# Reordering the last pair of a matmul kernel: one third product and the direct columns moved ahead, final block added and stored in two halves

## The chip, the cores and the metric

The kernel runs on one core of one Trainium2 chip. The metric is the device time of one execution in microseconds. Beside it stands the span of a profiled execution, which is some 1.8 us shorter (363.13 against 361.35 us for the profiled run of before). The profiled run can lie above the median of the timed ones, as here (363.13 against 362.59 us).

## The reference

```python
def setup_inputs():
    batch, seq, hidden = 16, 512, 768
    return {
        "x": np.random.randn(batch, seq, hidden).astype(np.float32),
        "w_qkv": np.random.randn(hidden, 3 * hidden).astype(np.float32),
    }

def reference(x, w_qkv):
    qkv = np.matmul(x, w_qkv)
    hidden = x.shape[-1]
    q, k, v = qkv[..., :hidden], qkv[..., hidden:2*hidden], qkv[..., 2*hidden:]
    return np.stack([q, k, v], axis=0).astype(np.float32)
```

That is 8192 rows of x by 768, times a 768 x 2304 matrix. The output, 75.5 MB, is split into three.

## The kernel before

The rows are worked in 32 pairs of 128-row tiles. Of the 2304 columns, 2048 are done in two "quads" (a and b) of 2 x 512 columns. A quad is a block product with seven products in place of eight; product n is `do(u, n)`. The other 256 columns, the "direct" ones, are plain products (`rem`). Within a quad, products 1, 6, 7 and 4 accumulate one after another in the same PSUM bank `u.x` (PSUM is the memory that the products are written to), and ScalarE reads that bank between them; 5 and 3 share `u.y`; VectorE adds.

```python
    def do(u, n):
        ...
        elif n == 7:
            product(u, 7, u.x, False)
            nc.scalar.activation(c22, u.x[:], ident)
            nc.vector.tensor_tensor(c22, c22, u.y[:], op=add)
        elif n == 4:
            product(u, 4, u.x, False)
            nc.scalar.activation(c21, u.x[:], ident)
        elif n == 3:
            product(u, 3, u.y, False)
            nc.vector.tensor_tensor(c12, c12, u.y[:], op=add)
```

The last pair has a function of its own, which stores each block as soon as it is done. A block is 128 x 512 values, 256 KB. `store_cols` makes two stores of 128 KB of it where it crosses from one output tensor to the next.

```python
        def rem_stored(r):
            ps = bank()
            rem_row(p, r, ps[:, :REM])
            o = or_pool.tile([P, 2, REM], fp32, name="orem")
            nc.scalar.activation(o[:, 0, :], ps[:, :REM], ident)
            row = (2 * p + r) * P
            nc.scalar.dma_start(out_flat[1, row:row + P, ...], o[:, 0, :])   # cut

        do(a, 1); do(b, 1); do(a, 2); do(a, 6); do(b, 2); do(b, 6)   # lines joined
        for u in (a, b):
            store_cols(u, 0, 0, CB, nc.sync)
        for u in (a, b):
            do(u, 5)
            do(u, 7)
            store_cols(u, 1, CB, 2 * CB, nc.sync)
        do(a, 4)
        store_cols(a, 1, 0, CB, nc.scalar)
        rem_stored(0)
        do(b, 4)
        store_cols(b, 1, 0, CB, nc.scalar)
        for u in (a, b):
            do(u, 3)
            store_cols(u, 0, CB, 2 * CB, nc.sync)
        rem_stored(1)
```

Of the kernel before, what the change touches and what calls it, by code (L numbers as in the profile page):

```python
# [10 lines left out]
def kernel(  # L11
# [20 lines left out]
    nc = tc.nc  # L32
# [10 lines left out]
    CB = 512  # L43
# [7 lines left out]
    add = mybir.AluOpType.add  # L51
# [149 lines left out]
    def product(u, n, ps, start):  # L201
        t1, t2, t3, t4 = ts[u.q]
        if n <= 2:
            h = (n - 1) * KH
            lhs = [xb[u.p][:, h + j, :P] for j in range(KH)]
            rhs = [b1[u.q][:, h + j, :] for j in range(KH)]
        else:
            k, t = {3: (4, b22[u.q][:]), 4: (0, t4), 5: (1, t1), 6: (2, t2), 7: (3, t3)}[n]
            lhs = [sr[u.p][:, k, j, :] for j in range(KH)]
            rhs = [t[:, j, :] for j in range(KH)]  # L210
        for j in range(KH):
            nc.tensor.matmul(  # L212
                ps[:], lhs[j], rhs[j],
                start=(start and j == 0), stop=(j == KH - 1), skip_group_check=True,
            )

    def bank():
        return ps_pool.tile([P, CB], fp32, name="ps")

    def do(u, n):  # L220
        c11, c12 = u.o[:, 0, :CB], u.o[:, 0, CB:]
        c21, c22 = u.o[:, 1, :CB], u.o[:, 1, CB:]
        if n == 1:
            u.x = bank()
            product(u, 1, u.x, True)
            nc.scalar.activation(c11, u.x[:], ident)  # L226
        elif n == 2:
            u.z = bank()
            product(u, 2, u.z, True)
            nc.vector.tensor_tensor(c11, c11, u.z[:], op=add)  # L230
        elif n == 6:
            product(u, 6, u.x, False)
            nc.scalar.activation(c12, u.x[:], ident)  # L233
        elif n == 5:
            u.y = bank()
            product(u, 5, u.y, True)
# [10 lines that stand above are left out]
# [13 lines left out]
    def rem_row(p, r, ps):  # L260
        for j in range(KT):
            nc.tensor.matmul(  # L262
                ps, xb[p][:, j, r * P:(r + 1) * P], w_rem[j // KH][:, j % KH, :],
                start=(j == 0), stop=(j == KT - 1), skip_group_check=True,
            )
# [30 lines left out]
    def store_cols(u, r, lo, hi, eng):  # L296

        c = Q_OFF[u.q] + lo
        end = Q_OFF[u.q] + hi
        while c < end:  # L300
            n = min(end, (c // H + 1) * H)
            row = (2 * u.p + r) * P
            eng.dma_start(  # L303
                out_flat[c // H, row:row + P, c % H:c % H + n - c],
                u.o[:, r, c - Q_OFF[u.q]:n - Q_OFF[u.q]],
            )
            c = n

    def last(a, b):

        p = a.p
# [6 lines that stand above are left out]
            row = (2 * p + r) * P  # L318
            nc.scalar.dma_start(out_flat[1, row:row + P, R_OFF - H:R_OFF - H + REM], o[:, 0, :])  # L319

        do(a, 1)
        do(b, 1)
        do(a, 2)
        do(a, 6)
        do(b, 2)
        do(b, 6)
        for u in (a, b):
            store_cols(u, 0, 0, CB, nc.sync)
        for u in (a, b):
            do(u, 5)  # L330
            do(u, 7)
            store_cols(u, 1, CB, 2 * CB, nc.sync)
        do(a, 4)
        store_cols(a, 1, 0, CB, nc.scalar)
        rem_stored(0)
        do(b, 4)
        store_cols(b, 1, 0, CB, nc.scalar)
        for u in (a, b):
            do(u, 3)
            store_cols(u, 0, CB, 2 * CB, nc.sync)  # L340
        rem_stored(1)


    NS = 3
# [113 lines left out]
    for p in range(NS, NP):  # L458
        def early():
            if p + 1 < NP:  # L460
                transpose(p + 1)
                round_x(p + 1)
                sums_x(p + 1)
            if p + 2 < NP:
                load_x(p + 2, nc.scalar)

        if p < NP - 1:
            two(quad(p, 0), quad(p, 1), early)
        else:
            last(quad(p, 0), quad(p, 1))  # L470
# [30 lines left out]
```

## Time and profile before

| what | value | how to read it |
|---|---|---|
| median time | 362.59 us (3 runs, 362.5 to 362.67) | |
| span of the profile | 361.35 us | first to last instruction |
| TensorE busy | 353.4 us, 98% | no pause worth naming |
| last pair's first matmul | 345.98 us | what comes before it is not changed |
| last matmul's end | 356.96 us | |
| last store's issue | 357.49 us, on ScalarE's queue | |
| last packet written | 359.52 us | from the trace's packet records |
| last semaphore complete | 359.87 us | then SyncE's waits and two barriers |

The prediction shows the timeline of this tail. One more view is the view of busy time by stretch. The columns are the stretch, its length, the busy time of five engine tracks (PE, the TensorE matmuls; PEld, its weight loads; DVE, VectorE; ACT, ScalarE; POOL, GpSimd), the granted clock, the DMA engines' busy share and their GB/s. A share slightly above 1 means that packets of one engine overlap.

```profile
356.00:356.50 0.50, 0.50 (x6) 0.34 (x5) 0.50 (x2) 0.12 (x1) 0.00 (x0) 1.00 1.01 375
356.50:357.00 0.50, 0.46 (x5) 0.17 (x2) 0.50 (x1) 0.00 (x0) 0.00 (x0) 1.00 0.57 195
357.00:357.50 0.50, 0.00 (x0) 0.00 (x0) 0.02 (x1) 0.39 (x1) 0.00 (x0) 1.00 1.02 356
357.50:358.00 0.50, 0.00 (x0) 0.00 (x0) 0.00 (x0) 0.00 (x0) 0.00 (x0) 1.00 1.08 377
...
359.00:359.50 0.50, 0.00 (x0) 0.00 (x0) 0.00 (x0) 0.00 (x0) 0.00 (x0) 1.00 0.85 295
```

The DMA engines are full from 357.0 on, with one hollow, a pause between stores, just ahead (share 0.57). No compute engine is busy after 357.5.

### The profile page before, as it was taken

To read this page: it belongs to the slowest core of one execution; us is meant where nothing else is said; L and a number is where in the kernel's file an instruction comes from. 1 tells how busy PE (TensorE), PEld (TensorE's weight loads), DVE (VectorE), ACT (ScalarE), POOL (GpSimd) and SP (SyncE) were. 2 spreads that over 40 slices of the span, in tenths; PEclk is the share of its full clock that TensorE was granted. 3 is DMA by queue.
4 is the path that set the end of the run, shared out by engine and by line. 5 is a ranking of instruction groups with operands and counts; after the bars stand their busy time and mean duration, and the time that the engine had idled before them with its cause. 6 is when DMAs were issued, how large, how long until landed. Compare 5 with 4: busy or idle time off the path is not lost.

```text
span 361.3 us, 5221 instructions
## 1 busy us (share of the span) xinstructions
PE 353.4 (98%) x1765; PEld 251.0 (69%) x1797; DVE 224.4 (62%) x239; ACT 182.9 (51%) x304; POOL 173.9 (48%) x180
## 2 busy tenths in 40 slices
PE   8999999999999999999999999999999999999995
PEld 3644577777777777777777777777777777777763
DVE  3499826765566765566675565676556676556642
ACT  4547555455454545454545445455545454545452
POOL 0001861746664445664445665444665444666410
PEclk9999999999999999999999999999999999999999
DMA  7999869988898999899899999998989899999666
GB/s 298 405 388 373 286 221 359 331 289 295 278 328 301 294 273 294 276 324 315 280 280 290 281 308 309 291 289 278 292 288 321 295 300 271 297 272 339 264 261 232
DMA packets 80617, 108.08 MB, mean 299 GB/s; under 512 B 4816, under 2 KB 60368, under 8 KB 80592
## 3 DMA queue, kind: packets, MB, share of 16 engines
q1 hardware_dynamic: 65184, 96.35, 80.8%
q10 hardware_dynamic: 15408, 11.41, 9.6%
q8 instruction: 14, 0.23, 0.3%
q14 instruction: 11, 0.09, 0.1%
HBM read 32.24 MB, written 75.50 MB: 298 GB/s over the span
## 4 chain that ended last, share of the span: by engine, by line
PE 96%; ACT 1%; issue 1%; ACTq 0%; DVE 0%
PE ps L212 75%; PE ps L262 11%; PE ps L385 9%; PE ps L365 1%; PE ps L167 1%; ACT o L243 0%; ACTq L303 0%; ACT xb L147 0%; ACT orem L317 0%; DVE xb L145 0%; ACT xc L147 0%; ACTq L319 0%; DVE zero L346 0%; ACTq L317 0%
## 5 line engine op out<-in xcount | busy, mean ns | idle before, releaser
L212 PE MATMUL ps<-t,s 128*128 128x512 f32 x696 | 173.8, 398 | 0.0
L212 PEld LDWEIGHTS ps<-t,s 128*128 128x128 f32 x696 | 130.7, 188 | 29.7
L175 POOL CAST xb<-xf 128x1536 bf16<-128x1536 f32 x29 | 43.8, 1510 | 168.3 <-DVE xf L130 156.0
L240 DVE TENSOR_TENSOR o<-o,ps 128x512 f32<-128x512 f32 x58 | 39.9, 688 | 91.2 <-ACT o L239 91.2
L130 DVE STREAM_TRANSPOSE xf<-xin 128x1536 f32<-128x1536 f32 x29 | 85.5, 2950 | 3.7 <-DMA out_dram<-orem 2.1
L212 PE MATMUL ps<-b,xb 128*128 128x512 bf16 x320 | 82.4, 380 | 1.5
L239 ACT ACTIVATE o<-ps 128x512 f32<-128x512 f32 x58 | 34.8, 600 | 44.2 <-PE ps L212 44.2
L212 PEld LDWEIGHTS <-xb 128*128 128x128 bf16 x348 | 31.7, 98 | 35.6 <-issue 7.3
L233 ACT ACTIVATE o<-ps 128x512 f32<-128x512 f32 x58 | 34.9, 601 | 42.1 <-PE ps L212 39.4
L246 DVE TENSOR_TENSOR o<-o,ps 128x512 f32<-128x512 f32 x58 | 39.9, 688 | 21.3 <-PE ps L212 20.2
L212 PE MATMUL ps<-b,s 128*128 128x512 f32 x174 | 48.7, 389 | 0.0
L262 PE MATMUL ps<-w_rem,xb 128*128 128x256 bf16 x384 | 47.2, 273 | 0.0
L243 ACT ACTIVATE o<-ps 128x512 f32<-128x512 f32 x58 | 34.7, 599 | 24.1 <-PE ps L212 21.3
L226 ACT ACTIVATE o<-ps 128x512 f32<-128x512 f32 x58 | 34.7, 598 | 23.8 <-DVE o L246 20.6
L262 PEld LDWEIGHTS <-xb 128*128 128x128 bf16 x384 | 37.4, 98 | 11.2 <-issue 0.5
L230 DVE TENSOR_TENSOR o<-o,ps 128x512 f32<-128x512 f32 x58 | 36.5, 673 | 5.4 <-PE ps L212 4.1
L212 PEld LDWEIGHTS ps<-b,s 128*128 128x128 f32 x174 | 32.7, 188 | 6.8
L184 POOL TENSOR_TENSOR s<-s,xf 128x384 fp32r<-128x384 f32 x29 | 30.0, 1035 | 2.3
L183 POOL TENSOR_TENSOR s<-xf 128x384 fp32r<-128x384 f32 x29 | 30.9, 1064 | 0.0
L185 POOL TENSOR_TENSOR s<-xf 128x384 fp32r<-128x384 f32 x29 | 29.5, 1017 | 0.0
L187 POOL TENSOR_TENSOR s<-xf,s 128x384 fp32r<-128x384 f32 x29 | 29.5, 1016 | 0.0
L272 ACT ACTIVATE orem<-ps 128x512 f32<-128x512 f32 x31 | 18.5, 598 | 20.7 <-PE ps L262 19.5
(36 smaller groups left out, 129.4 us busy)
## 6 DMA issues: line engine op xcount, KB each, us to landing
out_dram<-o SPq DMA_DIRECT2D x62, 768.0 KB, 4.8
out_dram<-o SPq DMA_DIRECT2D x65, 256.0 KB, 4.1
xin<-in_x_dram SPq DMA_DIRECT2D x62, 192.0 KB, 6.9
xin<-in_x_dram ACTq DMA_DIRECT2D x54, 192.0 KB, 4.4
out_dram<-orem SPq DMA_DIRECT2D x31, 256.0 KB, 5.7
st<-in_w_qkv_dram SPq DMA_DIRECT2D x6, 768.0 KB, 13.1
xin<-in_x_dram SPq DMA_DIRECT2D x3, 768.0 KB, 5.7
st<-in_w_qkv_dram SPq DMA_DIRECT2D x6, 256.0 KB, 6.1
```

What stands on the lines that cost most here:

```text
L130: nc.vector.transpose(t[:].rearrange("p j (g b) -> p g j b", b=G), xin.pop(p)[:].rearrange("p g (a j) -> p g j a", a=G),)
L175: nc.gpsimd.tensor_copy(out=xb[p][:], in_=xf[p][:])
L212: nc.tensor.matmul(ps[:], lhs[j], rhs[j], start=(start and j == 0), stop=(j == KH - 1), skip_group_check=True,)
L226: nc.scalar.activation(c11, u.x[:], ident)
L230: nc.vector.tensor_tensor(c11, c11, u.z[:], op=add)
L233: nc.scalar.activation(c12, u.x[:], ident)
L239: nc.scalar.activation(c22, u.x[:], ident)
L240: nc.vector.tensor_tensor(c22, c22, u.y[:], op=add)
L243: nc.scalar.activation(c21, u.x[:], ident)
L246: nc.vector.tensor_tensor(c12, c12, u.y[:], op=add)
L262: nc.tensor.matmul(ps, xb[p][:, j, r * P:(r + 1) * P], w_rem[j // KH][:, j % KH, :], start=(j == 0), stop=(j == KT - 1), skip_group_check= ...
L385: nc.tensor.matmul(ps[n][:], xb[p][:, j, r * P:(r + 1) * P], w[:, j, :], start=(j == 0), stop=(j == KT - 1), skip_group_check=True,)
```

## The change

The intent is to end on compute work whose output can leave in pieces. The first quad's third product and both direct blocks go ahead of the last two products; fourth blocks are stored from Sync; the final block is added and stored in two halves, so that the first half is under way while the second is added.

```diff
-        do(a, 1)
-        do(b, 1)
-        do(a, 2)
-        do(a, 6)
-        do(b, 2)
-        do(b, 6)
+        for n in (1, 2):
+            for u in (a, b):
+                do(u, n)
         for u in (a, b):
             store_cols(u, 0, 0, CB, nc.sync)
-        for u in (a, b):
-            do(u, 5)
-            do(u, 7)
-            store_cols(u, 1, CB, 2 * CB, nc.sync)
+        do(a, 6)
+        do(a, 5)
+        do(b, 6)
+        do(a, 7)
+        store_cols(a, 1, CB, 2 * CB, nc.sync)
+        do(b, 5)
+        do(b, 7)
+        store_cols(b, 1, CB, 2 * CB, nc.sync)
         do(a, 4)
-        store_cols(a, 1, 0, CB, nc.scalar)
+        store_cols(a, 1, 0, CB, nc.sync)
+        do(a, 3)
+        store_cols(a, 0, CB, 2 * CB, nc.sync)
         rem_stored(0)
+        rem_stored(1)
         do(b, 4)
-        store_cols(b, 1, 0, CB, nc.scalar)
-        for u in (a, b):
-            do(u, 3)
-            store_cols(u, 0, CB, 2 * CB, nc.sync)
-        rem_stored(1)
+        store_cols(b, 1, 0, CB, nc.sync)
+        product(b, 3, b.y, False)
+        for lo in (CB, CB + CB // 2):
+            hi = lo + CB // 2
+            part = b.o[:, 0, lo:hi]
+            nc.vector.tensor_tensor(part, part, b.y[:, lo - CB:hi - CB], op=add)
+            store_cols(b, 0, lo, hi, nc.scalar)
```

## The prediction

> **What bounds the kernel now.** I read the page first: engine shares, then the chain that ended last.
>
> ```profile
> PE 353.4 (98%) x1765; PEld 251.0 (69%) x1797; DVE 224.4 (62%) x239; ACT 182.9 (51%) x304; POOL 173.9 (48%) x180
> PE 96%; ACT 1%; issue 1%; ACTq 0%; DVE 0%
> ```
>
> TensorE is busy without a break from start to end. The diff leaves its work alone: the same 67 matmuls stand in the last pair, in another order. So the change can only act after the last pair begins at 345.98 us, and I read the timeline of the tail next (start, duration, engine, line):
>
> ```profile
> 353.97 0.94 PE L212 MATMUL ps<-t,s 128*128 128x512 f32 x3
> 354.21 0.39 ACTq L303 DMA_DIRECT2D out_dram<-o  x1
> ...
> 354.75 1.54 PE L212 MATMUL ps<-b,s 128*128 128x512 f32 x6
> 355.11 0.37 ACTq L319 DMA_DIRECT2D out_dram<-orem  x1
> 355.53 0.60 ACT L243 ACTIVATE o<-ps 128x512 f32<-128x512 f32 x1 [0.45 <-ACT orem L317]
> 355.64 1.37 DVE L246 TENSOR_TENSOR o<-o,ps 128x512 f32<-128x512 f32 x2 [1.42 <-PE ps L212]
> 356.13 0.83 PE L262 MATMUL ps<-w_rem,xb 128*128 128x256 bf16 x6
> 356.15 0.82 ACTq L303 DMA_DIRECT2D out_dram<-o  x2
> 357.08 0.39 ACT L317 ACTIVATE orem<-ps 128x256 f32<-128x256 f32 x1 [0.95 <-PE ps L262]
> 357.49 0.34 ACTq L319 DMA_DIRECT2D out_dram<-orem  x1
> ```
>
> The last matmul ends at 356.96, the last store is issued at 357.49, but the span ends at 361.3. What fills the last 3.8 us is seen in the view of busy time by stretch (the two last figures are DMA share and GB/s) and in SyncE's waits:
>
> ```profile
> 354.00:356.00 2.00, 2.00 (x11) 1.56 (x9) 0.58 (x2) 1.04 (x3) 0.00 (x0) 1.00 0.71 268
> 356.00:358.00 2.00, 0.96 (x8) 0.51 (x6) 1.02 (x2) 0.51 (x2) 0.00 (x0) 1.00 0.92 326
> 358.00:360.00 2.00, 0.00 (x0) 0.00 (x0) 0.00 (x0) 0.00 (x0) 0.00 (x0) 1.00 0.76 276
> SPq L496 <- DMA out_dram<-o: 1.9, 1, 1.9
> ```
>
> From 357.0 to 359.5 the 16 DMA engines are full: in half-microsecond stretches of the DMA view the two queues' shares add up to 1.02, 1.08, 1.14, 1.04 and 0.86. The packets show the stores served one after another: each 128 KB store in 1 KB rows takes 0.345 us of all engines (8 packets of 43 ns on each), each 256 KB store in 2 KB rows 0.65 us (8 of 81 ns). The last packet is written at 359.51, its semaphore is complete at 359.87, and SyncE's remaining waits and two barriers take 1.48 us to 361.35. **So the tail is set by a queue of stores, not by the last product.** The last store shows it: issued at 357.49, its first packet moves at 359.03, after 1.54 us, while stores issued into an idle system needed 0.83 (354.25 to 355.08) and 0.85 us (356.15 to 357.00). Some 0.7 us is standing in line.
>
> **What the Trainium skill says.**
> - "DMA: Bandwidth & Descriptors", Issuing engines are not separate DMA queues: DMAs of the Sync and Scalar queues run on the same 16 engines, and a second issuer saves only sequencer time. The trace agrees, as the two shares add up to about 1. So moving stores from the Scalar to the Sync queue gains no bandwidth.
> - Same page, Latency and other measured facts: first byte some 600 ns after a hardware-generated issue. The trace has 0.83 to 0.85 us from the issue's start, and I use that.
> - "Perfetto Trace Analysis", DMA Optimizations: splitting a DMA may let part of it start sooner if the DMA engines are generally idle. Here they are not idle, so the halves have little to win.
> - "VectorE: DVE Perf Modes", The TRN2 errata: an fp32 tensor_tensor takes (N+151)/0.96 ns. For N=512 that is 691 ns; the trace has 688. For the new halves, N=256, it gives an estimate of 424 ns.
>
> **The change part by part.**
>
> *TensorE order.* The trace gives slots of 0.227 us for an fp32 matmul, 0.216 for a bf16 one, 0.109 for a 256-column one. A change between bf16 and fp32 costs 0.01 to 0.02 us, and the new order has three fewer, worth about 0.04 us. Laying the slots out from 345.98: seventh products of both quads at their old places, third product of the first quad 353.35 to 354.03, direct columns 354.03 to 355.35, fourth product to 356.05, third product to 356.74. With the drain of 0.16 us it is done at 356.90, against 356.96 before. No bank waits: every evacuation ahead of an accumulating product ends at least 0.5 us before it.
>
> *Stores that come earlier.* The first quad's third block is added 354.22 to 354.91 and stored at about 355.15 and 355.5, before at 356.36 and 356.75. The second direct block is issued at about 356.25, before at 357.49.
>
> *Stores that come later.* The fourth block of the first quad waits behind another issue on Sync, to 354.7 (before 354.21). ScalarE's line now is: direct block 0 (0.385, issue 0.35 to 0.42), direct block 1 (the same), and only then the fourth block of the second quad, because each issue holds ScalarE and the next ACTIVATE starts 0.05 to 0.10 us after it. So its product is ready at 356.2 but it is read from about 356.6 to 357.2; its two 128 KB stores go out at 357.25 and 357.65. Before they went out at 356.15 and 356.53: **1.1 us later**.
>
> *The final block.* Halves added 356.94 to 357.36 and to 357.79 (2 x 0.424; whole: 0.688). Issues at about 357.4 and 357.85, the second a third of a microsecond after the last issue of before.
>
> *Sum on the path that sets the end.* From 355.08 on, both kernels still have the same 1536 KB to write. Before: 3 x 0.65 + 6 x 0.345 = 4.02 us of engine time, plus a gap of 0.27 us at 356.73 to 357.00 and 0.13 of spread at the end, which gives 359.5. After: 2 x 0.65 + 8 x 0.345 = 4.06 us, since the final block's rows are now 1 KB. The first 1024 KB (one 256 KB block each of two quads, the four stores of third block and direct columns) are issued in time and run from 355.08 to 357.76. The next store is issued at 357.25 and moves at 358.1, so a gap of 0.34 us. Then four stores of 0.345 without a gap, to 359.48, plus 0.13: 359.6. Against 359.51 that is +0.1. Compilation shows that SyncE waits at the end for the last semaphore one place later in its list, which returns 0.065 us. Net: +0.03 us, which I round to nothing. Since the ScalarE line may run 0.1 us better than laid out, I put the time at 362.5 against 362.59.
>
> **The rivals.**
> - *The intended gain.* If the queue has drained when the last half is issued, that half needs only 0.85 + 0.48 + 0.35 us to its semaphore: 357.85 gives 359.53, 0.34 us earlier than 359.87, with the 0.065 some 0.4 us: 362.2. For it: 512 KB of stores leave earlier. Against it: four stores come within 0.6 us at the end, and 1.38 us of engine time from 358.1 can't end before 359.5.
> - *ScalarE as the new wait.* If its issues take 0.44 us, as one of before did beside a Sync issue, the fourth block comes another 0.1 to 0.2 us later, and all four stores with it: 362.7 to 362.8. The last half also has to wait for the semaphore of the first direct store, eight stores back; I have that landing near 357.4 to 357.7, so just in time, but a slip there adds to the end.
> - *A better packing.* If the fourth block is read at 356.25 as soon as its product ends, the gap vanishes and the packed end is 359.27: 362.3. Against it is the order of ScalarE's instructions.
>
> **Range and chances.** The whole tail after TensorE is under 5 us; 2% is 7.25 us. Nothing here can reach that in either direction. The three cases span 362.2 to 362.8, the runs of before 362.50 to 362.67. Predicted 362.5 us, range 362.1 to 362.9; faster by over 2% 0.005, same 0.99, slower 0.005.
>
> **What would show it right or wrong.** Right: the last matmul ends at 356.9 (within 0.1); the L243 ACTIVATE of the second quad starts at 356.5 to 356.7, after both direct blocks' issues; the last two Sync stores are issued after 357.1; the DMA view is full again from about 358.0 to 359.5, with a hollow ahead of it; the last packet falls in 359.3 to 359.7. Wrong: a last packet before 359.2, which would mean that the stores don't stand in line as I have it; or an ACTIVATE of the fourth block at 356.3; or a half add far from 0.42 us; or a hollow in TensorE at a bank.

## The result, and the profile after

| | before | changed |
|---|---|---|
| median time | 362.58 us (6 runs, 362.5 to 363.3) | 362.74 us (6 runs, 362.6 to 363.12) |
| ratio | | 1.0003, 95% interval 0.999 to 1.0015 |
| span | 361.35 us | 361.35 us |
| last pair's first matmul | 345.98 | 345.92 |
| last matmul's end | 356.96 | 356.90 |
| last store's issue | 357.49 | 357.83 |
| last packet written | 359.52 | 359.58 |

A ratio is the mean time of one kernel's fast runs over that of the other's fast runs in the same rounds, so it is not quite the ratio of the medians. The change does nothing measurable to the time.

The page of the changed kernel, engine shares and the chain that ended last by engine:

```profile
PE 355.0 (98%) x1797; PEld 251.1 (69%) x1797; DVE 224.4 (62%) x240; ACT 182.5 (50%) x304; POOL 173.4 (48%) x180
PE 98%; DVE 0%; ACT 0%; issue 0%; DVEq 0%
```

TensorE's busy time seems to have grown by 1.6 us, but so has the number of recorded matmuls, 1797 against 1765: 32 records were missing from the first trace, none were added by the change. This is no finding.

The timeline of the changed kernel's tail (start, duration, engine, line, operation, and what ended the idle time; ACTq is ScalarE's sequencer, which issues DMAs):

```profile
354.88 0.38 ACT L317 ACTIVATE orem<-ps 128x256 f32<-128x256 f32 x1 [0.75 <-PE ps L262]
...
355.30 0.38 ACTq L319 DMA_DIRECT2D out_dram<-orem  x1
355.77 0.38 ACT L317 ACTIVATE orem<-ps 128x256 f32<-128x256 f32 x1 [0.51 <-PE ps L262]
...
356.04 0.86 PE L212 MATMUL ps<-b,s 128*128 128x512 f32 x3
356.19 0.37 ACTq L319 DMA_DIRECT2D out_dram<-orem  x1
356.60 0.60 ACT L243 ACTIVATE o<-ps 128x512 f32<-128x512 f32 x1 [0.45 <-PE ps L212]
356.94 0.75 DVE L346 TENSOR_TENSOR o<-o,ps 128x256 f32<-128x256 f32 x2 [2.04 <-PE ps L212]
357.39 0.82 ACTq L303 DMA_DIRECT2D out_dram<-o  x2
```

Read it by ScalarE's line: direct block, issue, direct block, issue, and only at 356.60 the fourth block of the second quad (L243). Its product was complete 0.4 us earlier. The bracket names PE as what ended the wait, but the engine's own DMA issue at 356.19 to 356.56 sits right before. In the kernel before, the same ACTIVATE starts at 355.53.

The changed kernel's busy time by stretch, answering to the lines shown of before:

```profile
356.50:357.00 0.50, 0.40 (x2) 0.00 (x0) 0.06 (x1) 0.40 (x1) 0.00 (x0) 1.00 1.10 385
357.00:357.50 0.50, 0.00 (x0) 0.00 (x0) 0.50 (x2) 0.20 (x1) 0.00 (x0) 1.00 1.07 369
357.50:358.00 0.50, 0.00 (x0) 0.00 (x0) 0.19 (x1) 0.00 (x0) 0.00 (x0) 1.00 0.55 191
358.00:358.50 0.50, 0.00 (x0) 0.00 (x0) 0.00 (x0) 0.00 (x0) 0.00 (x0) 1.00 0.89 313
358.50:359.00 0.50, 0.00 (x0) 0.00 (x0) 0.00 (x0) 0.00 (x0) 0.00 (x0) 1.00 1.08 377
359.00:359.50 0.50, 0.00 (x0) 0.00 (x0) 0.00 (x0) 0.00 (x0) 0.00 (x0) 1.00 1.02 355
```

The hollow ahead of 357.0 is gone (0.57 became 1.10), and another stands a microsecond later (1.08 became 0.55). The stores have the same bytes, and the pause has moved.

### The profile page after: what moved, and what is told of

The parts are those of the page before. It is cut to its first block, busy times and chain, and to the rows that moved or that the text cites. A ratio compares the mean times of both kernels' runs of the same rounds, so it can differ in the third digit from the quotient of the medians.

```text
span 361.3 us, 5257 instructions
## 1 busy us (share of the span) xinstructions
PE 355.0 (98%) x1797; PEld 251.1 (69%) x1797; DVE 224.4 (62%) x240; ACT 182.5 (50%) x304; POOL 173.4 (48%) x180
## 4 chain that ended last, share of the span: by engine, by line
PE 98%; DVE 0%; ACT 0%; issue 0%; DVEq 0%
PE ps L212 76%; PE ps L262 12%; PE ps L391 9%; PE ps L371 1%; PE ps L167 1%; ACT xb L147 0%; DVE xb L145 0%; DVE o L346 0%; ACT xc L147 0%; DVEq L502 0%; DVE zero L352 0%
## 5 line engine op out<-in xcount | busy, mean ns | idle before, releaser
L212 PE MATMUL ps<-b,xb 128*128 128x512 bf16 x348 | 84.7, 380 | 0.0
L243 ACT ACTIVATE o<-ps 128x512 f32<-128x512 f32 x58 | 34.7, 598 | 24.1 <-PE ps L212 21.8
```

The costliest lines, as they stand in the source:

```text
L212: nc.tensor.matmul(ps[:], lhs[j], rhs[j], start=(start and j == 0), stop=(j == KH - 1), skip_group_check=True,)
```

## The experiments

Theory: **the end is set by the stores standing in line for the 16 DMA engines, plus any hollow ahead of them**; the change closes one hollow (the first quad's third block is stored earlier) and opens another (ScalarE reads the second quad's fourth block late). Main rival: **the last store's own way sets the end**, so what counts is when the last half is added and issued.

One thing came out first, which decides how to read all of them. The start of the last pair differed between profiles by 0.74 us, from 345.35 to 346.09, and the difference is there already at the first fp32 product (48.33 to 49.09 us), far from the change. So I count the tail from the first matmul of the last pair, written +. Below is the sum over all profiles; "fourth read" is the start of the second quad's fourth ACTIVATE.

| kernel | fourth read | last issue | last packet | end of span | median time | before, same rounds |
|---|---|---|---|---|---|---|
| before | +9.55 | +11.51 | +13.54 | +15.37 | 362.58 | |
| changed | +10.68 | +11.90 | +13.66 | +15.42 | 362.74 | 362.58 |
| third_only | +9.81 | +11.74 | +13.29 | +15.12 | 362.28 | 362.86 |
| direct_only | +10.40 | +11.94 | +14.05 | +15.88 | 363.31 | 362.86 |
| direct_sync | +10.32 | +12.01 | +13.63 | +15.51 | 363.14 | 362.86 |
| spread | +9.68 | +11.59 | +13.25 | +15.07 | 362.36 | 362.86 |
| whole | +10.68 | +11.73 | +13.76 | +15.66 | 362.94 | 362.96 |
| no_fourth_store (wrong) | +10.68 | +11.90 | +13.31 | +15.20 | 362.93 | 362.96 |
| direct_last | +9.80 | +12.22 | +13.56 | +15.31 | 362.52 | 362.96 |
| spread2 | +10.36 | +11.44 | +13.20 | +15.03 | 362.23 | 362.96 |
| fourth_between | +9.80 | +11.91 | +13.35 | +15.11 | 362.36 | 362.79 |
| before_again | +9.55 | +11.52 | +13.54 | +15.36 | 362.88 | 362.79 |
| after_again | +10.68 | +11.90 | +13.67 | +15.41 | 362.90 | 362.79 |
| spread2_again | +10.36 | +11.44 | +13.19 | +15.02 | 362.47 | 362.79 |

The last three rows repeat kernels: their tails agree with the first profiles within 0.02 us, while run-up and time scatter by several tenths. The tail is the sharper measure.

### third_only: the third product ahead, alone

```diff
 (kernel before)
         do(a, 4)
         store_cols(a, 1, 0, CB, nc.scalar)
+        do(a, 3)
+        store_cols(a, 0, CB, 2 * CB, nc.sync)
         rem_stored(0)
         do(b, 4)
         store_cols(b, 1, 0, CB, nc.scalar)
-        for u in (a, b):
-            do(u, 3)
-            store_cols(u, 0, CB, 2 * CB, nc.sync)
+        do(b, 3)
+        store_cols(b, 0, CB, 2 * CB, nc.sync)
         rem_stored(1)
```

> The kernel before, with one part of the change alone: the third product of the first quad, its add and its stores go right behind the fourth product of the first quad; the rest, with the second direct block last, stays. Queue theory (the end is set by stores in line plus the hollow ahead of them): the two stores of that block leave at about 355.0 and 355.3 instead of 356.36 and 356.75, the hollow before 357.0 closes, the 1536 KB run from 355.05 without a pause, last packet at 359.2 (before 359.51), 0.3 us faster: about 362.25 us. Rival (the last store's own way sets the end, 2.0 us from its issue to its last packet): the second direct block still is the last store, issued at 357.5 to 357.7, so the last packet stays at 359.5 to 359.7 and the time at 362.6.

Last packet at +13.29, against +13.54 before, although the last store was issued 0.23 us later than before. The ratio is 0.9988 (0.9975 to 1.0). Its busy time by stretch (this profile's last pair starts 0.63 us sooner than that of before, at 345.35):

```profile
356.00:356.50 0.50, 0.33 (x4) 0.05 (x1) 0.39 (x1) 0.00 (x0) 0.00 (x0) 1.00 1.10 383
356.50:357.00 0.50, 0.00 (x0) 0.00 (x0) 0.00 (x0) 0.32 (x1) 0.00 (x0) 1.00 1.08 377
357.00:357.50 0.50, 0.00 (x0) 0.00 (x0) 0.00 (x0) 0.06 (x1) 0.00 (x0) 1.00 1.03 361
357.50:358.00 0.50, 0.00 (x0) 0.00 (x0) 0.00 (x0) 0.00 (x0) 0.00 (x0) 1.00 1.11 424
```

No hollow is left. A later issue and an earlier end are what the line of stores predicts, and not what the rival predicts. This part of the change, alone, was worth 0.25 us.

### direct_only: both direct blocks ahead, alone

```diff
 (kernel before)
         rem_stored(0)
+        rem_stored(1)
         do(b, 4)
         ...
-        rem_stored(1)
```

> The kernel before, with another part alone: both direct blocks go ahead of the fourth product of the second quad; third products stay last, whole, stored on Sync. Queue theory: ScalarE reads the fourth product of the second quad only at about 356.6, after both direct blocks' issues, its stores leave at about 357.25 and 357.65 and move at 358.1; a hollow of some 0.6 us stands before about 357.8, and the last packet comes at 359.9 (before 359.51): 0.4 us slower, about 362.95 us. Rival (the last store's own way): the last store is the third block of the second quad, issued at about 357.7 against 357.49, so 0.2 us slower at most; second rival (ScalarE's order doesn't matter): no change.

Last packet at +14.05, 0.51 us later than before (expected 0.4). The ratio is 1.0014 (1.0 to 1.0028). ScalarE's timeline and the hollow behind it, from two views of this kernel:

```profile
355.22 0.37 ACTq L319 DMA_DIRECT2D out_dram<-orem  x1
355.69 0.38 ACT L317 ACTIVATE orem<-ps 128x256 f32<-128x256 f32 x1 [0.50 <-PE ps L212]
356.10 0.34 ACTq L319 DMA_DIRECT2D out_dram<-orem  x1
356.49 0.60 ACT L243 ACTIVATE o<-ps 128x512 f32<-128x512 f32 x1 [0.42 <-PE ps L212]
```

```profile
357.00:357.50 0.50, 0.05 (x1) 0.00 (x0) 0.50 (x2) 0.09 (x1) 0.00 (x0) 1.00 0.70 244
357.50:358.00 0.50, 0.00 (x0) 0.00 (x0) 0.28 (x1) 0.00 (x0) 0.00 (x0) 1.00 0.04 14
358.00:358.50 0.50, 0.00 (x0) 0.00 (x0) 0.00 (x0) 0.00 (x0) 0.00 (x0) 1.00 1.04 371
```

The fourth block is read at 356.49, behind the second issue, and the DMA engines then stand idle for half a microsecond (share 0.04). The rival had 0.2 us at most; ScalarE's order not mattering had nothing. So the two parts of the change work against each other: -0.25 us from the third product, +0.51 us from the direct blocks, each measured alone at the last packet. Their sum is +0.26, and the whole change has +0.12. Most of the rest is the change's third part, the two halves: without them (whole, below) the changed kernel's last packet is at +13.76, which is +0.22 from before. What then remains, 0.04 us, covers the stores' new queues, the new order of the earlier products and how the parts act on one another; it was not taken apart.

### direct_sync: direct blocks issued from Sync

```diff
 (changed kernel, in rem_stored)
-            nc.scalar.dma_start(out_flat[1, row:row + P, ...], o[:, 0, :])
+            nc.sync.dma_start(out_flat[1, row:row + P, ...], o[:, 0, :])
```

> The changed kernel, with one edit: the two direct blocks are stored from Sync, so ScalarE issues nothing ahead of the fourth product of the second quad. Queue theory: that ACTIVATE starts at 356.2 to 356.3 (in the changed kernel 356.60), its two stores leave near 356.85 and 357.25, the hollow at 357.7 to 358.06 goes, the last packet falls at 359.25 (changed kernel 359.58), 0.3 us faster than the changed kernel, about 362.4 us. Rival (the last half add and its issue at 357.8 set the end): the issue of the last half stays where it is or 0.1 earlier, so the last packet stays at 359.5 to 359.6 and the time at 362.7.

A miss. The ACTIVATE did start early: 355.82, which is +10.32 against +10.68. But the last packet came at +13.63, no better than the changed kernel's +13.66, and not at the expected +13.3. Sync's queue in this kernel, from its timeline (two issues in each line):

```profile
355.67 0.89 SPq L319 DMA_DIRECT2D out_dram<-orem  x2
356.65 0.92 SPq L303 DMA_DIRECT2D out_dram<-o  x2
```

Six stores of 128 KB now leave one queue, and their issues start 0.49 us apart on average (354.68, 355.14, 355.67, 356.16, 356.65, 357.12 in the trace), while the DMA engines need 0.345 us for each. From the second direct block on, the packets come when the queue delivers them: that block was issued from 356.16 to 356.56 and moved its first packet at 357.11, and the next was issued from 356.65 to 357.07 and moved at 357.6. About 0.15 us of the engines' time is lost before each of the two: their share falls to 0.76 in the half-microsecond from 357.0 and to 0.81 in the next, from 1.02 just before and 1.09 just after. The line of stores was there as expected; what I had left out is that one queue can't feed it. The rival had the same number, +13.6, but for a reason that did not occur: the last issue did not stay where it was, it moved 0.11 us later.

### fourth_between: the order of ScalarE alone

```diff
 (changed kernel)
         rem_stored(0)
-        rem_stored(1)
         do(b, 4)
         store_cols(b, 1, 0, CB, nc.sync)
+        rem_stored(1)
```

> The changed kernel with the fourth product of the second quad moved between the two direct blocks, nothing else: same stores on the same queues, same halves. It parts the change's two orders: ScalarE then reads the fourth product ahead of the second direct block. Counted from the first matmul of the last pair. Queue theory: that ACTIVATE starts at +9.8 (changed kernel +10.68), its stores leave at about +10.5 and +10.9, the stores run without a hollow, last packet at +13.3 to +13.4 (changed kernel +13.66). Rival (the last half's own way): the last half's add and issue stay at +11.35 and +11.9, so +13.66 stays.

This is the cleanest test. All stores, their sizes and their queues are those of the changed kernel, and the last half is issued at +11.91 as there (+11.90). Only the fourth product of the second quad now comes between the direct blocks. Timeline of ScalarE and busy time by stretch (its last pair starts at 345.39):

```profile
354.76 0.38 ACTq L319 DMA_DIRECT2D out_dram<-orem  x1
355.18 0.60 ACT L243 ACTIVATE o<-ps 128x512 f32<-128x512 f32 x1 [0.45 <-PE ps L212]
355.72 0.39 ACT L317 ACTIVATE orem<-ps 128x256 f32<-128x256 f32 x1
```

```profile
356.50:357.00 0.50, 0.00 (x0) 0.00 (x0) 0.50 (x2) 0.00 (x0) 0.00 (x0) 1.00 1.08 375
357.00:357.50 0.50, 0.00 (x0) 0.00 (x0) 0.17 (x1) 0.00 (x0) 0.00 (x0) 1.00 1.10 385
357.50:358.00 0.50, 0.00 (x0) 0.00 (x0) 0.00 (x0) 0.00 (x0) 0.00 (x0) 1.00 1.10 379
```

The block is read at +9.80 in place of +10.68, the hollow goes, and the last packet comes at +13.35, 0.31 us earlier than in the changed kernel, with the last issue unmoved. That excludes the rival as the cause of the changed kernel's end. It does not say how much further the closing of hollows can go: the run below measures 1.42 us for a last half that has no fourth block ahead of it, and from +11.91 that makes +13.33, so at +13.35 the line and the last half's own way end together. The ratio to before is 0.9989 (0.9976 to 1.0003).

### no_fourth_store: fewer bytes in the line

```diff
 (changed kernel; wrong on purpose, one block stays unwritten)
         do(b, 4)
-        store_cols(b, 1, 0, CB, nc.sync)
```

> The changed kernel without the two stores of the second quad's fourth block (128 KB each): wrong on purpose, that block stays unwritten. ScalarE, TensorE and the add of the halves are untouched. Queue theory: the halves' stores, issued at +11.47 and +11.9, find the engines free; the first packet of the last one moves 0.85 to 0.95 us after its issue (changed kernel 1.27), and the last packet comes at +13.15 to +13.25 instead of +13.66: 0.4 us faster than the changed kernel. Rival (the last half's own way sets the end): the same +13.66 and the same time, since neither its add nor its issue has moved.

The last issue is again at +11.90, and the last packet comes at +13.31 instead of +13.66, so 0.35 us earlier: that much was standing in line behind the fourth block's 256 KB. I expected +13.15 to +13.25. The last half was issued in 0.39 us, and 1.42 us passed from the issue's start to the last packet. The time did not show it (362.93 against 362.96 before, ratio 1.0003, interval 0.9987 to 1.0018); with that scatter of the run-up it could not settle 0.3 us.

### whole: the halves undone

```diff
 (changed kernel)
-        product(b, 3, b.y, False)
-        for lo in (CB, CB + CB // 2):
-            ...
-            nc.vector.tensor_tensor(part, part, b.y[:, lo - CB:hi - CB], op=add)
-            store_cols(b, 0, lo, hi, nc.scalar)
+        do(b, 3)
+        store_cols(b, 0, CB, 2 * CB, nc.scalar)
```

> The changed kernel with the final block added whole and stored by one DMA from Scalar in place of two halves. All times counted from the first matmul of the last pair, since the run-up to it varied by 0.7 us between the four profiles of the first set. Changed kernel: last packet at +13.66. Queue theory: the hollow at +11.8 to +12.1 and the four stores' turn stay; the last block costs 0.65 in place of 2 x 0.345 us of engine time: last packet at +13.6, within 0.1 of the changed kernel, and the time within 0.1 us of it. Rival (the halves let the end come sooner, as the change intends): a whole add ends 0.3 us after the first half and the 256 KB store starts only then, so the last packet would come 0.2 to 0.3 us later, +13.9.

Last packet at +13.76, between the two expectations: 0.10 us later than with halves, where I had expected 0.06 earlier and the rival some 0.24 later. So the halves do buy 0.1 us at the last packet. The single store was issued at 357.32 to 357.67 and moved its first packet at 358.21 (0.51 us after the issue's end is 358.18), where most engines had been free for 0.1 us; a first half, issued 0.27 us sooner in the changed kernel, would have been there. The span's end came 0.24 us later, since SyncE's waits and barriers after the last semaphore took 1.54 us here and 1.41 in the changed kernel. The times, 362.94 and 362.96 us, show no difference.

### direct_last: second direct block last again

```diff
 (changed kernel)
         rem_stored(0)
-        rem_stored(1)
         do(b, 4)
         ...
             store_cols(b, 0, lo, hi, nc.scalar)
+        rem_stored(1)
```

> The changed kernel with one line moved: the second direct block is last again, behind the halves. Queue theory: the fourth product of the second quad is read right after its end (ACTIVATE at +9.9, changed kernel +10.68), its stores leave at +10.5 and +10.9 on Sync, the hollow goes. But ScalarE now issues both halves before it reads the direct block, so that block's store leaves only at about +12.1: last packet at +13.4, where the store's own way (0.34 issue, 0.51 to the first packet, 0.48 for 128 KB) and the line are about even. 0.2 to 0.25 us faster than the changed kernel, 0.1 faster than before. Rival (ScalarE's issues ahead of the fourth product cost nothing): same as the changed kernel or slower.

The fourth block is read at +9.80 as expected, but the last packet comes only at +13.56 (expected +13.4). Here the last store's own way does set the end: ScalarE issues both halves first, reads the direct block at +11.81 and issues it at +12.22; 0.34 us of issue, 0.51 to the first packet and 0.49 for the packets make +13.56. With the hollow closed, the next limit lies 0.1 us below the changed kernel's end, and it is the one the rival named. Its median time, 362.52 against 362.96 us before in the same rounds, looks 0.4 us better, though its tail ends no sooner than that of before (+13.56 and +13.54): so much can come from the run-up alone.

### spread and spread2: an order that beats both

```diff
 (changed kernel -> spread)
+        rem_stored(0)
         do(a, 4)
-        store_cols(a, 1, 0, CB, nc.sync)
+        store_cols(a, 1, 0, CB, nc.scalar)
         do(a, 3)
         store_cols(a, 0, CB, 2 * CB, nc.sync)
-        rem_stored(0)
-        rem_stored(1)
         do(b, 4)
-        store_cols(b, 1, 0, CB, nc.sync)
-        product(b, 3, b.y, False)
-        for lo in (CB, CB + CB // 2):      # and the four lines under it
+        store_cols(b, 1, 0, CB, nc.scalar)
+        do(b, 3)
+        store_cols(b, 0, CB, 2 * CB, nc.sync)
+        rem_stored(1)

 (spread -> spread2: third products ahead of fourth products)
+        do(a, 3)
+        store_cols(a, 0, CB, 2 * CB, nc.sync)
         do(a, 4)
         store_cols(a, 1, 0, CB, nc.scalar)
-        do(a, 3)
-        store_cols(a, 0, CB, 2 * CB, nc.sync)
-        do(b, 4)
-        store_cols(b, 1, 0, CB, nc.scalar)
         do(b, 3)
         store_cols(b, 0, CB, 2 * CB, nc.sync)
+        do(b, 4)
+        store_cols(b, 1, 0, CB, nc.sync)
```

> A candidate to beat both: the changed kernel's order, but the first direct block ahead of the first quad's fourth product, the second direct block last again, the final block whole, fourth blocks stored from Scalar, direct blocks from Scalar. Queue theory: a store of 128 KB now fills the pause after 354.7, the third block of the first quad leaves at about 355.6 and 356.0, no hollow is left after 355.9, and the last packet comes at 359.05 (before 359.51): about 362.1 us. If only the last store's own way counts, it is issued at 357.5 as before, and the last packet stays at 359.5: 362.6 us.

> A second candidate to beat both: as the candidate of the first set (last packet at +13.25 there), but third products ahead of fourth products, with the fourth block of the second quad stored from Sync, so that the add of the third block on VectorE is done earlier and ScalarE issues only three stores. What the first set showed is in this estimate: an issue takes 0.33 us alone and 0.42 to 0.46 beside another, and the first packet moves 0.51 us after the issue's end. Last packet at +13.06, 0.5 us ahead of the kernel before (+13.54); time 362.1 us against 362.6. Rival (the first candidate's +13.25 is the floor of this tail): +13.25 again.

Last packets at +13.25 and +13.20 (expected +13.07, which is 359.05 less the 345.98 of before, and +13.06). Both are the right way, with six to seven tenths of the expected gain: stores that leave both queues at once take longer to issue (0.42 to 0.46 us), so the line is not always fed. spread2 is 0.34 us ahead of the kernel before in the tail, and 362.23 us against 362.96 in its rounds (ratio 0.9984, interval 0.9972 to 0.9997). Far from 2%, but the best version here.

### before_again, after_again, spread2_again: does the tail repeat?

Same kernels as before, changed and spread2, profiled again on one chip.

> The kernel before, profiled once more, to see how far its tail repeats. If the tail is as deterministic as the engines' slots suggest: last packet at +13.54 after the first matmul of the last pair, within 0.05, whatever the run-up (345.98 us in its first profile).

> The changed kernel, profiled once more on the same chip as the other three: last packet at +13.66 within 0.05, the fourth block's ACTIVATE at +10.68, and a time within 0.2 us of the kernel before. If the run-up to the last pair differs from 345.92 us by several tenths while the tail stays, the spread of the times comes from the run-up.

> The better candidate once more, on the same chip as the kernel before and the changed kernel: last packet at +13.20, within 0.05, so 0.34 us ahead of the kernel before and 0.46 ahead of the changed kernel in the tail; time some 0.3 us below the kernel before, if the run-up is the same.

Last packets at +13.54, +13.67 and +13.19, all within 0.02 us of their first profiles. The last pair started at 345.35, 346.01 and 345.35. The times were 362.88, 362.90 and 362.47 us; spread2's interval this time reaches over 1 (0.9977 to 1.0002). So the candidate's 0.34 us is sure in the tail and only likely in the time.

## Why the prediction was right

The range held (362.74 in 362.1 to 362.9). That alone says little: the changed kernel's second median, 362.90, lies on the edge of that range, and the run-up scatters by nearly as much as the range is wide (0.74 and 0.8 us). The steps say more, and most of them held. Where they are compared below by the clock of the profile, the measured times have a run-up that is 0.06 us shorter (345.92 against the 345.98 laid out from), so they agree to within some 0.1 us and not to the hundredth; that 356.90 was forecast and met for the last matmul's end is such luck.

- *TensorE can't be the source.* Right, though the count is misread: the last pair has 54 matmuls (14 products of 3, 12 for the direct columns), and the 67 that the prediction names are a longer stretch of the chain, from 338.29 us on. No sum rests on it. The last pair takes +10.98 us to its last matmul's end in both kernels, and there is no wait at a bank. The 0.04 us that I gave to fewer changes of data type did not come; 0.006 us did.
- *Earlier stores.* Laid out at 355.15 and 355.5 for the third block and 356.25 for the second direct block, measured at 355.10, 355.56 and 356.19.
- *ScalarE's line holds back the fourth block.* Laid out from 356.6 to 357.2, measured 356.60 to 357.20. Its stores were to go at 357.25 and 357.65 and went at 357.22 and 357.61. fourth_between shows what this costs: 0.31 us come back when only that order is changed, more than the 0.12 us that the whole change lost.
- *The final block.* Issues at 357.39 and 357.83, laid out at 357.4 and 357.85. The second half ended at 357.69 and not at 357.79, because the second add starts 0.08 us before the first one's record ends; it changed nothing, since ScalarE was still issuing the first half.
- *The sum.* A hollow until the next store moves at 358.1 (measured 358.06), then four stores in line to 359.6 (measured 359.58).
- *The end.* SyncE's waits after the last semaphore took 1.409 us in place of 1.482, so 0.07 us less (0.065 laid out). The tail as a whole is 0.05 us longer than before; the net I had was +0.03. Counted by the last packet, the change costs 0.12 us (+0.1 laid out).
- *The size that was off.* The point, 362.5, leaned to the fast side "since the ScalarE line may run 0.1 us better than laid out". It did not run better, and the sign was wrong: the sum had the tail 0.03 us longer, the point had the time 0.09 us shorter.

Of the rivals, the better packing was right in its number: with the fourth block read early it had the packed end at 359.27. fourth_between's +13.35, on the changed kernel's run-up of 345.92, is 359.27. In part that is luck, since by then the last half's own way ends within 0.03 us of the line, and the estimate had only the line. The intended gain did not come because the last half still stood in line, behind three stores issued in the 0.6 us before it: no_fourth_store shows 0.35 us of that in the changed kernel. The reading of the Trainium skill's "Perfetto Trace Analysis", DMA Optimizations, on splitting was right in direction only: with the engines not generally idle the halves won little, but whole shows 0.10 us at the last packet, so not nothing.

What is open: what the stores' new queues and the new order of the earlier products do alone (together with the interplay of the parts, 0.04 us at the last packet), and where in the first 48 us the run-up's 0.74 us come from.

## What to carry to other kernels

At the end of a kernel whose outputs leave as fast as they are made, count the DMA engines' time of the last stores and look for pauses in it; a reordering that only moves the pause gains nothing. In this tail ScalarE both reads PSUM and issues stores, and an issue of 0.37 us delayed its next read by as much (the read came at +10.68, and at +10.32 with the issues on Sync); putting the read of the 256 KB block ahead of that of a 128 KB one was worth 0.31 us. So look which read an issue holds up. To judge a change of a few tenths of a microsecond, count from an event just ahead of the changed part, not from the start of the span.

## What the Trainium skill lacked or had wrong

- "DMA: Bandwidth & Descriptors", Issuing engines are not separate DMA queues, says that the sequencer time for an issue is usually small relative to the DMA itself. For 128 KB stores it is not: direct_sync's issues start 0.49 us apart on one queue, against 0.345 us of engine time for each store, and the engines paused twice for it.
- Same page, Latency and other measured facts: it gives some 600 ns to the first byte. Here the first packet moved 0.51 us after the end of the issue and 0.83 to 0.85 us after its start where nothing stood in line.
- "Perfetto Trace Analysis", DMA Instruction — HWDGE (DVE, Sync), has a wait for the descriptor generator in the issue's record, but no figure. In these tails an issue takes 0.33 to 0.37 us alone and up to 0.47 us when it overlaps or directly follows another.
- "VectorE: DVE Perf Modes", The TRN2 errata: it has (N+151)/0.96 ns checked at N of 512 and 2048. It holds for N=256 too, 424 ns against 421 and 415 measured in the changed kernel. Two such adds in a row started 0.34 us apart.
- No page that I used gives how far the time of one kernel scatters before a given point: here the start of the last pair scattered by 0.74 us over 14 profiles, and the last packet, counted from there, by at most 0.02 us between two profiles of one kernel (three kernels).
